# Output-projection weights and two mixers' outputs kept as split pairs, linear attention woven into projections, token halves

## The chip, the cores and the metric

One Trainium2 chip, one core of it. Five engines work from queues of their own, each in its own fixed order: PE (matrix products), DVE (vector), ACT (scalar), POOL (GpSimd), SP (which here issues the DMAs). The metric is device microseconds of one launch; the median of the runs is compared.

## What is computed

One layer of a streaming encoder on 1024 tokens of width 1024, all fp32.

```python
h = rmsnorm(x, ln1)
z = h @ w_in                      # split among three token mixers
y_pool = pool_mixer(u_pool, w_pool, pool_scale)        # trailing means over 2, 4, 8, 16, minus identity, a product per group
y_gla  = gla_mixer(gq, gk, gv, gg, ga, w_a_up, b_a, gla_gn)   # gated linear attention, 4 heads of 64, chunks of 64
y_fox  = fox_mixer(fq, fk, fv, ff, b_f)                # softmax attention with forgetting, 8 heads of 64, causal
x = x + concat(y_pool, y_gla, y_fox) @ w_o             # widths 256, 256, 512
h = rmsnorm(x, ln2)
gate, up = split(h @ w_gu); x = x + (silu(gate) * up) @ w_down
return rmsnorm(x, ln_f)
```

In the linear attention, per head: `S_t = diag(alpha_t) S_{t-1} + k_t^T v_t`, `o_t = q_t S_t`, by chunks: products within a chunk (`att = q_in k_in^T`, masked, times v), and q times the state before the chunk; then a normalisation per head and a gate `silu(g)`.

## The kernel before

Each large fp32 matrix product runs as three products of a split pair: an operand is rounded to a form that PE takes at full rate (`hi`, by ACT), the remainder (`lo`) is a subtraction (DVE or POOL), and PE adds hi·hi, hi·lo and lo·hi (`gemm`, L138). `split_w` (L111 to L113) loads and splits a weight; `load_w` uses buffers of small rings, `load_g` large ones. Names end in `h` and `l` for the two parts.

A scheduler orders each engine's queue by its own model of time, within the dependencies and within the buffers: tiles from `G` share large SBUF slots that are handed out again in order of release (`free`), tiles from `R` sit in rings, PSUM banks belong to tags (`s`, `pt`, `o`, `gm`). Code order is a priority, not the final order.

The stages, with the microseconds of the profiled execution:

- 0 to 72: first norm, transposes into `hT`, gates (`psg`), the pool mixer's input projections `zp0`, `zp1`.
- 72 to 118: keys and queries of the linear attention (`gla_qk`): projections `zgk0`, `zgq0`, `zgk1`, `zgq1`, 48 products of 512 columns each (`project`, L253). DVE and POOL prepare decays `bc`, `d1`, `d2`; `pk` turns the keys.
- 118 to 203: the pool mixer's sums (`ps`, `pd`) and products `py`; `gla_state` (small products `pkv`, L325, and the running state `St` on DVE, L330); values of the attention `psv0`; `gla_out` per head pair: gate projection `zgg`, scores `pat` (L353), masked into `attb` (L355), outputs `po` (L364 within a chunk, L368 with the state), normalisation `on`, turn `pot`, gate `gy`. Outputs go to DRAM (`mixd`) in fp32.
- 203 to 498: forgetting attention, four head pairs p = 0 to 3 (`fox_item`: scores `s`, softmax `pb` with the scaling L499 on POOL, turns `pt` L510, `pp`, outputs `o` L524), with the projections `zq`, `zk`, `psv1` in between, and for p = 3 the first half of the output projection, `pxa` (k = 0 to 3: pool and linear attention's outputs), as filler. `load_mix` reads rows of `mixd` into `mr` and splits them (ACT L562, POOL L563). `w_o` is loaded and split here: k = 0 to 3 with POOL, the rest with DVE. `fb` tiles hold the forget sums of one head.
- 498 to 560: second half `pxb` (k = 4 to 7), residual, second norm, its turns `n2pt` (L639).
- 560 to 977: gate and up products (L710, tiles `m`) by a scheme of seven products for a 2 by 2 block product; `left` prepares the left factors `hA`, `right` the weights, `start` begins a column block.
- 977 to 1202: down products (L916, `d`), again seven; POOL combines weights (`rw`, L808), which ACT and DVE split (`hw`, `lw`, L815, L816); at the end `final` normalises the tiles `c0` to `c7` and stores them (L883 to L887), and frees them.

Of the kernel before, what the change touches and what calls it, by code (L numbers as in the profile page):

```python
# [9 lines left out]
F32 = mybir.dt.float32  # L10
# [21 lines left out]
def tile_hybrid_block(ctx: ExitStack, tc, x, w_fv, w_gv, w_zt, w_o, w_gu, w_down, ln, w_pool, w_a3, chans, b_f, consts, out):  # L32
# [107 lines left out]


# [118 lines left out]
    decs, bcs = [], []  # L260
# [24 lines left out]
    def gla_qk(j):  # L285
        bc = bcs[j]
        b3 = e3(bc)
        dc = cst.tile([P, 16], F32, name=f"dec{j}")
        decs.append(dc)
        ACT.activation(dc, b3[:, :, 63], AF.Exp, scale=1.0 / 16)  # L290
        d1, d2, eq = G(f"d1_{j}"), R(f"d2_{j}"), G(f"eq{j}")
        POOL.tensor_tensor(out=e3(d1), in0=b3, in1=b3[:, :, 31:32].broadcast_to([P, 16, 64]), op=ALU.subtract)
        POOL.tensor_tensor(out=e3(d2), in0=b3[:, :, 63:64].broadcast_to([P, 16, 64]), in1=b3, op=ALU.subtract)
        ACT.activation(eq, d1, AF.Exp, scale=1.0 / 16)
        ACT.activation(d1, d1, AF.Exp, scale=-1.0 / 16)
        ACT.activation(d2, d2, AF.Exp, scale=1.0 / 16)
        ACT.activation(bc, bc, AF.Exp, scale=1.0 / 16)
        k_, q_ = R(f"gk{j}"), R(f"gq{j}")
        for csl, ps in project(8 + 2 * j, f"zgk{j}"):
            ACT.activation(k_[:, csl], ps, AF.Copy)  # L300
        DVE.tensor_tensor(out=d2, in0=k_, in1=d2, op=ALU.mult)
        DVE.tensor_tensor(out=d1, in0=k_, in1=d1, op=ALU.mult)
        for csl, ps in project(9 + 2 * j, f"zgq{j}"):
            ACT.activation(q_[:, csl], ps, AF.Copy, scale=0.125)
        DVE.tensor_tensor(out=eq, in0=q_, in1=eq, op=ALU.mult)
        POOL.tensor_tensor(out=bc, in0=q_, in1=bc, op=ALU.mult)
        kt = G(f"k2t{j}")
        for h in range(2):
            pt = PS("pt", f"pk{j}_{h}")
            for i in range(4):  # L310
                tb = 4 * h + i
                PE.transpose(pt[:, i * P:(i + 1) * P], d2[:, tb * P:(tb + 1) * P], ident)
            ACT.activation(kt[:, h * 512:(h + 1) * 512], pt, AF.Copy)
        return eq, d1, bc, kt

    def gla_state(j, kt):

        St = G(f"St{j}")
        POOL.memset(St[:, 0:64], 0.0)
        ps = [PS("s", f"pkv{j}_{q}") for q in range(2)]  # L320
        for n in range(15):
            tb, r = n // 2, slice(64 * (n % 2), 64 * (n % 2) + 64)
            o = ps[n % 2][:, (n // 2) * 64:(n // 2) * 64 + 64]
            for a in range(2):
                PE.matmul(o[64 * a:64 * a + 64], kt[r, tb * P + 64 * a:tb * P + 64 * a + 64],  # L325
                          gv[tb // 4][r, (tb % 4) * 256 + (2 * j + a) * 64:(tb % 4) * 256 + (2 * j + a + 1) * 64],
                          start=True, stop=True)
        for n in range(15):
            o = ps[n % 2][:, (n // 2) * 64:(n // 2) * 64 + 64]
            DVE.scalar_tensor_tensor(out=St[:, (n + 1) * 64:(n + 2) * 64], in0=St[:, n * 64:(n + 1) * 64],  # L330
                                     scalar=decs[j][:, n:n + 1], in1=o, op0=ALU.mult, op1=ALU.add)
        free(f"k2t{j}")
        return St

# [4 lines left out]
    def gla_out(j, qi, ki, qe, St):  # L339
        sg = R(f"sg{j}")  # L340
        for csl, ps in project(12 + j, f"zgg{j}"):
            ACT.activation(sg[:, csl], ps, AF.Silu)
        y = R(f"gy{j}")
        for c in range(2):
            pat = [PS("pt", f"pat{j}_{c}_{a}") for a in range(2)]
            po = [PS("s", f"po{j}_{c}_{a}") for a in range(2)]
            ab = attb[c]
            for i in range(4):
                tb = 4 * c + i
                tsl = slice(tb * P, (tb + 1) * P)  # L350
                for a in range(2):
                    r = slice(64 * a, 64 * a + 64)
                    PE.matmul(pat[a][:, i * P:(i + 1) * P], ki[r, tsl], qi[r, tsl], start=True, stop=True)  # L353
            for a in range(2):
                DVE.copy_predicated(ab[:, a * 512:(a + 1) * 512].rearrange("p (m t) -> p m t", t=P),  # L355
                                    gmask.rearrange("p (o t) -> p o t", o=1).broadcast_to([P, 4, P]),
                                    pat[a].rearrange("p (m t) -> p m t", t=P))
# [15 lines left out]
            for a in range(2):  # L373
                ACT.activation(o4[:, a], pv[a], AF.Square)
# [634 lines left out]
```

## Time and profile before

| what | value |
|---|---|
| median of three runs | 1199.56 us (1198.48 to 1200.44) |
| the profiled execution's own time | 1203.56 us |
| its span in the profile | 1201.8 us |
| granted PE clock, mean | 0.979 of full |
| busy: PE, PE weight loads, DVE, ACT, POOL | 1159.9, 974.8, 810.2, 530.9, 390.9 us |
| DMA | 126.34 MB, mean 105 GB/s |
| chain that ended last | PE 84%, DVE 5%, DMA 3%, issue 3%, POOL 3%, ACT 2% |

Busy time of PE is the time between a product's start and its modelled end: at half clock it counts the same work as twice the time. A row of a table of stages gives the length, the busy time of each engine with its count of instructions, the granted clock, the busy share of the DMA engines and GB/s. A row of the timeline gives start, length, engine, line, operation, tiles. A row of the waits says which engine waited for what: total, times, longest.

### The profile page before, as it was taken

What the parts mean: (1) busy time and instruction counts of PE and PEld (TensorE: products, weight loads), DVE (VectorE), ACT (ScalarE), POOL (GpSimd) and SP (SyncE); (2) the same over time, 40 slices, a digit from 0 to 9 for tenths busy, and PEclk for the clock granted to TensorE, in tenths of its full rate; (3) what the DMA queues carried; (4) which work ended last, traced back from release to release, by engine and by line L of the source; (5) the groups of instructions that cost most, each with busy time, mean ns of one, the idle gap of its engine ahead of it and who ended that gap; (6) DMA issues with size and microseconds to landing.
All of it is one profiled execution on the core that took longest, in us unless ns stands there. A gap on an engine that the chain in (4) does not pass through costs nothing.

```text
span 1201.8 us, 15933 instructions
## 1 busy us (share of the span) xinstructions
PE 1159.9 (97%) x5928; PEld 974.8 (81%) x5928; DVE 810.2 (67%) x1328; ACT 530.9 (44%) x965; POOL 390.9 (33%) x285
## 2 busy tenths in 40 slices
PE   6999999999999989899999999999999999999995
PEld 6878788889988778777888888888888888888874
DVE  7567612278748676468998768676776685766674
ACT  6362121257656745346444334443343344334353
POOL 2163122243333823331022220122202270660873
PEclk9999889899999999899999999999999999999998
DMA  6121111111122522221153331323224588333223
GB/s 244 35 71 53 54 35 53 36 55 47 47 62 77 169 91 97 79 105 53 53 155 112 111 120 65 131 93 118 95 90 148 214 322 288 109 96 118 63 97 140
DMA packets 53565, 126.34 MB, mean 105 GB/s; under 512 B 4792, under 2 KB 10344, under 8 KB 53488
## 3 DMA queue, kind: packets, MB, share of 16 engines
q1 hardware_dynamic: 53056, 123.75, 30.7%
q0 software_dynamic: 432, 1.57, 0.4%
q8 instruction: 46, 0.75, 0.3%
q14 instruction: 31, 0.25, 0.1%
HBM read 93.03 MB, written 32.28 MB: 104 GB/s over the span
## 4 chain that ended last, share of the span: by engine, by line
PE 84%; DVE 5%; DMA 3%; issue 3%; POOL 3%; ACT 2%; POOLq 0%; SPq 0%; ACTq 0%; DVEq 0%
PE m L710 35%; PE d L916 16%; PE pxa L138 4%; PE psv L138 3%; PE o L524 3%; PE pt L510 2%; PE s L484 1%; PE zq0p L138 1%; PE zgg0p L138 1%; PE s L485 1%; DMA mr<-mixd 1%; PE psg L138 1%; PE po L364 1%; PE zq3p L138 1%; PE zgg1p L138 1%
## 5 line engine op out<-in xcount | busy, mean ns | idle before, releaser
L710 PE MATMUL m<-hA_0h,wr 128*128 128x512 f32 x616 | 214.3, 390 | 0.6 <-ACT hr L641 0.5
L710 PE MATMUL m<-hA_1h,wr 128*128 128x512 f32 x616 | 214.6, 389 | 0.0
L710 PEld LDWEIGHTS m<-hA_0h,wr 128*128 128x128 f32 x616 | 115.6, 188 | 24.9 <-ACT hr L641 1.1
L710 PEld LDWEIGHTS m<-hA_1h,wr 128*128 128x128 f32 x616 | 115.7, 188 | 23.9
L916 PE MATMUL d<-hw,ha 128*128 128x512 f32 x308 | 120.0, 392 | 5.3 <-ACT hw L815 5.3
L710 PE MATMUL m<-hA_0l,wr 128*128 128x512 f32 x308 | 119.9, 389 | 1.7 <-DVE hA_0l L671 1.7
L916 PE MATMUL d<-lw,ha 128*128 128x512 f32 x308 | 120.4, 391 | 0.8 <-DVE lw L816 0.8
L710 PE MATMUL m<-hA_1l,wr 128*128 128x512 f32 x308 | 119.8, 389 | 0.0
L762 POOL TENSOR_TENSOR cg<-cu,cu 128x512 f32<-128x512 f32 x11 | 19.2, 1742 | 308.7 <-DVE cu L739 308.7
L916 PE MATMUL d<-hw,la 128*128 128x512 f32 x308 | 118.8, 391 | 0.0
L694 ACT ACTIVATE wr<-ws 128x512 fp32r<-128x512 f32 x110 | 69.5, 631 | 109.2 <-DVE ws L693 54.9
L695 DVE TENSOR_TENSOR wr<-ws,wr 128x512 fp32r<-128x512 f32 x110 | 75.9, 696 | 26.0 <-ACT wr L694 26.0
L816 DVE TENSOR_TENSOR la<-ra,ha 128x1024 fp32r<-128x1024 f32 (+1 forms) x42 | 58.2, 1392 | 29.0 <-ACT ha L815 21.5
L808 POOL TENSOR_TENSOR rw<-wd,wd 128x512 f32<-128x512 f32 x33 | 56.4, 1737 | 51.3 <-PE d L916 46.6
L916 PEld LDWEIGHTS d<-hw,ha 128*128 128x128 f32 x308 | 58.1, 189 | 17.8 <-ACT hw L815 5.7
L710 PEld LDWEIGHTS m<-hA_0l,wr 128*128 128x128 f32 x308 | 57.8, 188 | 14.2 <-DVE hA_0l L671 2.2
L916 PEld LDWEIGHTS d<-lw,ha 128*128 128x128 f32 x308 | 58.3, 189 | 13.3 <-DVE lw L816 1.2
L815 ACT ACTIVATE ha<-ra 128x1024 fp32r<-128x1024 f32 (+1 forms) x42 | 41.2, 987 | 61.6 <-DMA ra<-cd 56.0
L916 PEld LDWEIGHTS d<-hw,la 128*128 128x128 f32 x308 | 58.1, 189 | 12.1
L710 PEld LDWEIGHTS m<-hA_1l,wr 128*128 128x128 f32 x308 | 57.8, 188 | 12.1
L499 POOL TENSOR_TENSOR pb<-pb,rl 128x128 f32<-128x128 f32 (+3 forms) x32 | 38.1, 1196 | 83.4 <-DVE rl L496 66.5
L816 DVE TENSOR_TENSOR lw<-rw,hw 128x1024 fp32r<-128x1024 f32 (+1 forms) x30 | 45.7, 1535 | 27.3 <-ACT hw L815 27.2
(391 smaller groups left out, 2764.1 us busy)
## 6 DMA issues: line engine op xcount, KB each, us to landing
ra<-cd SPq DMA_DIRECT2D x35, 512.0 KB, 3.7
wu<-in_w_gu_dram SPq DMA_DIRECT2D x22, 512.0 KB, 4.3
wg<-in_w_gu_dram SPq DMA_DIRECT2D x22, 512.0 KB, 3.7
wd<-in_w_down_dram SPq DMA_DIRECT2D x22, 512.0 KB, 6.5
cd<-cg SPq DMA_DIRECT2D x11, 512.0 KB, 4.6
cd<-cs SPq DMA_DIRECT2D x11, 512.0 KB, 6.2
cd<-cu SPq DMA_DIRECT2D x11, 512.0 KB, 7.5
fb<-Fd SPq DMA_DIRECT2D x8, 512.0 KB, 4.5
```

The lines of the kernel that those rows point to most:

```text
L138: PE.matmul(ps, a, b, start=(n == 0), stop=(n == last))
L499: POOL.tensor_tensor(out=pb[:, 0:W], in0=pb[:, 0:W], in1=rl[:, 0:1].broadcast_to([P, W]), op=ALU.mult)
L510: PE.transpose(pt[:, o0:o0 + P], Pb[i][:, (2 * n + b) * P:(2 * n + b + 1) * P], ident)
L524: PE.matmul(*args, start=(kb == 0 and n_ == 0), stop=(last and n_ == 1))
L694: ACT.activation(hi, src, AF.Copy)
L695: e2.tensor_tensor(out=lo, in0=src, in1=f(hi), op=ALU.subtract)
L710: PE.matmul(ps, a, b, start=(n == 0), stop=(n == 11))
L762: POOL.tensor_tensor(out=t_[:, 0:512], in0=a11, in1=a12, op=ALU.add)
L808: POOL.tensor_tensor(out=raw_[:, j * 512:j * 512 + 512], in0=wd[h0, j0 + j][:, e0, :], in1=wd[h1, j0 + j][:, e1, :], op=op)
L815: ACT.activation(hi[:, sl], src, AF.Copy)
L816: DVE.tensor_tensor(out=lo[:, sl], in0=src, in1=f(hi[:, sl]), op=ALU.subtract)
L916: PE.matmul(banks[t], a[:, o], b[:, ns], start=(j0 + j == 0 and m == 0), stop=(j0 + j == NF // 2 - 1 and m == 2))
```

## The change

Five things.

1. Linear attention is written as a class `Gla` per head pair, whose small operations (turned keys, state, scores, outputs, turned outputs) are handed to the following projections and emitted between their terms (`woven`). The weights' `lo` parts of these projections are made on DVE instead of POOL. The four `attb` products of a part of `po` come first, then the state's. `pool_tile` stands ahead in the code.
2. `keep_mix`: the outputs of pool and linear attention are split once and stored as pairs (`mixs`); `load_mix` for k < 4 only loads.
3. `keep_wo`: the eight row blocks of `w_o` are loaded, split and stored as pairs (`wod`) after the first attention values in the code; `fetch_wo` loads pairs later.
4. Token halves: a half is now tokens 0 to 511 or 512 to 1023 (before: 0 to 255 with 512 to 767, and the others). The last head pair runs its query blocks in the order 1, 0, 3, 2 (before 3, 1, 2, 0). `pxb` goes through the token blocks 0 to 7; at block 4 the first left factors and the first column block of the FFN are started, and the rings of `wr` and `w` are given up earlier.
5. `free(f"c{tb}")` at the end of `final` is gone.

```diff
+    def woven(ps, terms, smalls=()):
+        done = 0
+        for i, ((ah, al), (bh, bl)) in enumerate(terms):
+            for n, (a, b) in enumerate(((ah, bh), (ah, bl), (al, bh))):
+                PE.matmul(ps, a, b, start=(i == 0 and n == 0), stop=(i == len(terms) - 1 and n == 2))
+            while done < len(smalls) and (done + 1) * len(terms) <= (i + 1) * len(smalls):
+                smalls[done]()
+                done += 1
...
+    def keep_mix(k, y):
+        hi, lo = R(f"mh{k}", F32R), R(f"ml{k}", F32R)
+        ACT.activation(hi, y, AF.Copy)
+        DVE.tensor_tensor(out=lo, in0=y, in1=f(hi), op=ALU.subtract)
+        SP.dma_start(mixs[k, :, 0], f(hi))
+        SP.dma_start(mixs[k, :, 1], f(lo))
+
+    def keep_wo(k):
+        hi, lo = load_g(w_o[k * P:(k + 1) * P, :], f"wos{k}", tag="G")
+        SP.dma_start(wod[k, :, 0], f(hi))
+        SP.dma_start(wod[k, :, 1], f(lo))
+        free(f"wos{k}h", f"wos{k}l")
+
+    def fetch_wo(k):
+        hl = G(f"wo{k}h", F32R), G(f"wo{k}l", F32R)
+        for h in range(2):
+            SP.dma_start(f(hl[h]), wod[k, :, h])
+        return hl
...
-    g0 = gla_qk(0)
-    g1 = gla_qk(1)
     pool_tile(1, us[1])
     pool_tile(0, us[0])
     free("misc")
-    st0 = gla_state(0, g0[3])
-    st1 = gla_state(1, g1[3])
-    V = fox_values(0)
-    gla_out(0, g0[0], g0[1], g0[2], st0)
-    gla_out(1, g1[0], g1[1], g1[2], st1)
+    A = Gla(0)
+    A.keys()
+    A.queries(((), A.turn_keys()))
+    A.gates((A.state(), A.within(0)))
+    B = Gla(1)
+    B.keys((A.within(1) + A.outputs(0), A.outputs(1) + A.turned(0)))
+    B.queries((A.turned(1), B.turn_keys()))
+    B.gates((B.state(), B.within(0)))
+    o_ = [B.outputs(0), B.outputs(1)]
+    V = fox_values(0, (B.within(1), o_[0][:1], o_[0][1:], o_[1][:1], o_[1][1:] + B.turned(0), B.turned(1), (), ()))
+    for k in range(8):
+        keep_wo(k)
...
-        for a, m in ([(a, m) for a in range(2) for m in range(4)] if p < 3 else [(a, m) for m in (3, 1, 2, 0) for a in range(2)]):
+        for a, m in ([(a, m) for a in range(2) for m in range(4)] if p < 3 else [(a, m) for m in (1, 0, 3, 2) for a in range(2)]):
...
-        o0 = (tb // 4) * 256 + (tb % 2) * P
+        o0 = (tb % 4) * P
...
-    ws = [load_g(w_o[k * P:(k + 1) * P, :], f"wo{k}", eng=POOL) for k in range(4)]
+    ws = [fetch_wo(k) for k in range(4)]
...
-    mixes = [load_mix(4, g) for g in (1, 0)][::-1]
-    for tb in (2, 3, 6, 7, 0, 1, 4, 5):
...
+    for tb in range(NT):
+        if tb == 2:
+            mixes[1] = load_mix(4, 1)
+        if tb == 4:
+            free(*[f"mix{k}_0" for k in range(4, 8)])
+            for i in (3, 5):
+                left(i, *lefts[i])
+            first.append(start(0))
+        out_proj(tb, xs[tb], mixes[tb // 4], ws, "pxb")
...
-        free(f"c{tb}")
```

In the rows below, the number at a name's end tells tiles apart, and `xN` is a run of N alike. PE, early in the linear attention, before: the last products of `zgk0p1` are followed by `zgq0p0`.

```order
L138 MATMUL zgk0p1_867<-hT3_1_0_97,zgk0h_836 128x512
L138 MATMUL zgk0p1_867<-hT3_1_1_98,zgk0h_836 128x512
L138 MATMUL zgk0p1_867<-hT3_1_0_97,zgk0l_837 128x512
L138 MATMUL zgq0p0_901<-hT0_0_0_83,zgq0h_896 128x512
L138 MATMUL zgq0p0_901<-hT0_0_1_84,zgq0h_896 128x512
L138 MATMUL zgq0p0_901<-hT0_0_0_83,zgq0l_897 128x512
```

After:

```order
L146 MATMUL zgk0p1_922<-hT3_1_0_97,zgk0h_891 128x512
L146 MATMUL zgk0p1_922<-hT3_1_1_98,zgk0h_891 128x512
L146 MATMUL zgk0p1_922<-hT3_1_0_97,zgk0l_892 128x512
L500 MATMUL py1_0_842<-pd1_837,misc_70 128x512
L500 MATMUL py1_1_845<-pd1_837,misc_70 128x512
L146 MATMUL zgq0p0_958<-hT0_0_0_83,zgq0h_953 128x512
L146 MATMUL zgq0p0_958<-hT0_0_1_84,zgq0h_953 128x512
```

The two products `py1` of the pool mixer, before at the place of 128 us, now stand between the two projections. On DVE, what stands ahead of `pd1`, which they read; before, from the row of `d2_0` on:

```order
L301 TENSOR_TENSOR d2_0_825<-gk0_833,d2_0_825 128x1024
L302 TENSOR_TENSOR d1_0_824<-gk0_833,d1_0_824 128x1024
L399 COPY ps2_1_1114<-u1_763 128x1
L400 TENSOR_TENSOR ps2_1_1114<-u1_763 128x1023
L305 TENSOR_TENSOR eq0_826<-gq0_834,eq0_826 128x1024
L399 COPY ps4_1_1117<-ps2_1_1114 128x2
L400 TENSOR_TENSOR ps4_1_1117<-ps2_1_1114 128x1022
L399 COPY ps2_0_1139<-u0_704 128x1
L400 TENSOR_TENSOR ps2_0_1139<-u0_704 128x1023
```

After, from the second scan on:

```order
L311 SCALAR_TENSOR_TENSOR bc1_699<-reset_653,la1_675 128x1024
L113 TENSOR_TENSOR zgq0l_954<-zgq0r_952,zgq0h_953 128x1024
L480 TENSOR_TENSOR ps2_1_824<-u1_765 128x1023
L479 COPY ps4_1_827<-ps2_1_824 128x2
L480 TENSOR_TENSOR ps4_1_827<-ps2_1_824 128x1022
L479 COPY ps8_1_830<-ps4_1_827 128x4
L480 TENSOR_TENSOR ps8_1_830<-ps4_1_827 128x1020
L479 COPY ps16_1_833<-ps8_1_830 64x8
L480 TENSOR_TENSOR ps16_1_833<-ps8_1_830 64x1016
L491 COPY ps8_1_830<-ps16_1_833 64x1024
L493 SCALAR_TENSOR_TENSOR pd1_837<-ps8_1_830,misc_70,u1_765 128x1024
```

The pool's sums follow the scan and the split `zgq0l` directly, with `pd1` in the same run. PE, one of the new groups (`zgk1p0` is the projection of the second pair's keys); before, a part of the same outputs in `zgg0`'s projection:

```order
L364 MATMUL po0_0_0_1566<-gv0_112,attb0_654 128x64
L368 MATMUL po0_0_0_1566<-St0_1158,bc0_695 64x64 x2
L364 MATMUL po0_0_1_1567<-gv0_112,attb0_654 128x64
L368 MATMUL po0_0_1_1567<-St0_1158,bc0_695 64x64 x2
L364 MATMUL po0_0_0_1566<-gv0_112,attb0_654 128x64
L368 MATMUL po0_0_0_1566<-St0_1158,bc0_695 64x64 x2
L364 MATMUL po0_0_1_1567<-gv0_112,attb0_654 128x64
L368 MATMUL po0_0_1_1567<-St0_1158,bc0_695 64x64
L138 MATMUL zgg0p0_1511<-hT0_0_0_83,zgg0h_1506 128x512
L138 MATMUL zgg0p0_1511<-hT0_0_1_84,zgg0h_1506 128x512
L368 MATMUL po0_0_1_1567<-St0_1158,bc0_695 64x64
```

After:

```order
L409 MATMUL pat0_1_0_1170<-eq0_882,d1_0_880 128x128
L409 MATMUL pat0_1_1_1171<-eq0_882,d1_0_880 128x128
L428 MATMUL po0_0_0_1194<-gv0_112,attb0_656 128x64
L428 MATMUL po0_0_1_1195<-gv0_112,attb0_656 128x64
L428 MATMUL po0_0_0_1194<-gv0_112,attb0_656 128x64
L428 MATMUL po0_0_1_1195<-gv0_112,attb0_656 128x64
L434 MATMUL po0_0_0_1194<-St0_1024,bc0_697 64x64 x2
L434 MATMUL po0_0_1_1195<-St0_1024,bc0_697 64x64 x2
L434 MATMUL po0_0_0_1194<-St0_1024,bc0_697 64x64 x2
L434 MATMUL po0_0_1_1195<-St0_1024,bc0_697 64x64 x2
L146 MATMUL zgk1p0_1163<-hT3_0_1_96,zgk1h_1158 128x512
L146 MATMUL zgk1p0_1163<-hT3_0_0_95,zgk1l_1159 128x512
```

A group is now four and eight `po` products of one part, with two products of the projection before the next group. At the end of the output projection PE's row now holds twelve products each of the FFN's first tiles `m0_3` and `m1_3` between the products of `pxb6`, `pxb7` and the last turns `n2pt6`, `n2pt7`; before, FFN products came in only after `n2pt4`, ahead of and behind `n2pt5`. POOL in the last stage, before:

```order
L808 TENSOR_TENSOR rw6_6_10220<-wd0_7_8946,wd1_7_8657 128x512
L808 TENSOR_TENSOR rw6_8_10257<-wd0_8_8984,wd1_8_8659 128x512
L808 TENSOR_TENSOR rw6_8_10257<-wd0_9_8986,wd1_9_8676 128x512
L878 TENSOR_TENSOR c0_8864<-c0_8864,lnfb_9255 128x512
L878 TENSOR_TENSOR c1_8866<-c1_8866,lnfb_9255 128x512
L101 TENSOR_TENSOR f0_r_10127<-f0_v_10126,mhalf_76 128x1
L878 TENSOR_TENSOR c2_8868<-c2_8868,lnfb_9255 128x512
L101 TENSOR_TENSOR f1_r_10140<-f1_v_10139,mhalf_76 128x1
L878 TENSOR_TENSOR c3_8870<-c3_8870,lnfb_9255 128x512
L101 TENSOR_TENSOR f2_r_10153<-f2_v_10152,mhalf_76 128x1
L101 TENSOR_TENSOR f3_r_10166<-f3_v_10165,mhalf_76 128x1
L808 TENSOR_TENSOR rw6_10_10294<-wd0_10_9024,wd1_10_8678 128x512
```

After:

```order
L865 TENSOR_TENSOR rw6_4_10233<-wd0_4_8954,wd1_4_8686 128x512
L865 TENSOR_TENSOR rw6_4_10233<-wd0_5_8956,wd1_5_8688 128x512
L865 TENSOR_TENSOR rw6_10_10344<-wd0_10_9074,wd1_10_8728 128x512
L865 TENSOR_TENSOR rw6_2_10152<-wd0_2_8897,wd1_2_8667 128x512
L865 TENSOR_TENSOR rw6_2_10152<-wd0_3_8899,wd1_3_8684 128x512
L865 TENSOR_TENSOR rw6_6_10270<-wd0_6_8994,wd1_6_8705 128x512
L865 TENSOR_TENSOR rw6_6_10270<-wd0_7_8996,wd1_7_8707 128x512
L865 TENSOR_TENSOR rw6_8_10307<-wd0_8_9034,wd1_8_8709 128x512
L865 TENSOR_TENSOR rw6_8_10307<-wd0_9_9036,wd1_9_8726 128x512
```

The combination `rw6_10` stood behind the last `c` tiles and now stands ahead of `rw6_2`. On SP, where nothing of the row is shown, 18 loads of 512 KB (pairs of `w_o`, pairs of mixes, `xa`), from `wo0h` on, stand ahead of the load `fb3_1`, which before stood after `wo0r`, `wo1r`, four `xa` and six halves of `mr`.

More of the change, by code (lines that the diff above doesn't have):

```diff
@@ L283, in decays @@
         free("fx")
[L285 to L333, printed above, removed]
@@ L643, in norm2 @@
         free(f"n2sq{tb}")
-    mixes = [load_mix(4, g) for g in (1, 0)][::-1]
-    for tb in (2, 3, 6, 7, 0, 1, 4, 5):
-        g = (tb // 2) % 2
-        out_proj(tb, xs[tb], mixes[g], ws, "pxb")
-        SP.dma_start(x3d[tb], xs[tb])
-        norm2(tb, xs[tb])
-        free(f"xa{tb}")
-        if tb in (7, 5):
-            free(*[f"mix{k}_{g}" for k in range(4, 8)])
-    free("wo6h", "wo6l", "wo7h", "wo7l", "ln2b")
-    idle.extend(rings.pop("wr") + rings.pop("w"))
-    hA = {}
-    def left(i, in0, in1=None, op=None):
-        hA[i] = []
-        for kp in range(2):
-            hi, lo = (G(f"hA{i}_{kp}{h}", F32R).rearrange("p (k t) -> p k t", k=2) for h in "hl")
-            src = raw[in0][kp]
-            if in1 is not None:
-                t_ = G(f"hs{i}{kp}").rearrange("p (k t) -> p k t", k=2)
-                DVE.tensor_tensor(out=t_, in0=src, in1=raw[in1][kp], op=op)
-                src = t_
-                free(f"hs{i}{kp}")
-            ACT.activation(hi, src, AF.Copy)
-            DVE.tensor_tensor(out=lo, in0=src, in1=f(hi), op=ALU.subtract)
-            hA[i].append((hi, lo))
     cd = dpool.tile([7, NF // 2, P, 512], F32, name="cd")
@@ L823, in prep, with left @@
             ready.append(ops)
+    hA = {}
+    def left(i, in0, in1=None, op=None):
+        hA[i] = []
+        for kp in range(2):
+            hi, lo = (G(f"hA{i}_{kp}{h}", F32R).rearrange("p (k t) -> p k t", k=2) for h in "hl")
+            src = raw[in0][kp]
+            if in1 is not None:
+                t_ = G(f"hs{i}{kp}").rearrange("p (k t) -> p k t", k=2)
+                DVE.tensor_tensor(out=t_, in0=src, in1=raw[in1][kp], op=op)
+                src = t_
+                free(f"hs{i}{kp}")
+            ACT.activation(hi, src, AF.Copy)
+            DVE.tensor_tensor(out=lo, in0=src, in1=f(hi), op=ALU.subtract)
+            hA[i].append((hi, lo))
     seen = []
@@ L841, in tile_hybrid_block @@
              6: (2, 0, ALU.subtract)}
-    first = [start(fi) for fi in range(2)]
+    mixes = [load_mix(4, 0), None]
+    first = []
+    for tb in range(NT):
[7 more added lines that the diff above has]
+        out_proj(tb, xs[tb], mixes[tb // 4], ws, "pxb")
+        SP.dma_start(x3d[tb], xs[tb])
+        norm2(tb, xs[tb])
+        free(f"xa{tb}")
+    free(*[f"wo{k}{h}" for k in range(4, 8) for h in "hl"], "ln2b", *[f"mix{k}_1" for k in range(4, 8)])
+    first.append(start(1))
     for i in (3, 5, 4, 1, 2, 7, 6):
-        left(i, *lefts[i])
+        if i not in (3, 5):
+            left(i, *lefts[i])
         if i == 7:
```

220 lines of the change are left out of this document (149 added, 71 removed).

## The prediction

> **What bounds the kernel now.** I read the stages first, then the granted clock, the waits of the PE queue, the chain at the end. The stages, one row each: length, busy time of PE, PEld, DVE, ACT, POOL with instruction counts, granted clock, DMA share, GB/s.
>
> ```profile
> 72.00:125.00 53.00, 52.50 (x266) 44.15 (x265) 33.30 (x23) 20.11 (x28) 30.44 (x12) 1.00 0.21 65
> 125.00:165.00 40.00, 38.11 (x356) 31.84 (x355) 19.53 (x58) 9.14 (x23) 3.39 (x3) 0.91 0.08 32
> 165.00:240.00 75.00, 75.00 (x385) 59.66 (x386) 15.67 (x29) 13.83 (x23) 18.23 (x12) 0.86 0.16 50
> 240.00:400.00 160.00, 159.72 (x1035) 144.38 (x1034) 116.50 (x293) 98.54 (x212) 60.78 (x55) 1.00 0.20 61
> 400.00:430.00 30.00, 25.00 (x135) 21.11 (x134) 21.20 (x49) 19.22 (x36) 22.37 (x17) 0.89 0.49 163
> 430.00:500.00 70.00, 64.22 (x364) 55.14 (x363) 43.28 (x89) 32.21 (x69) 19.27 (x20) 0.98 0.25 82
> 500.00:560.00 60.00, 57.28 (x272) 46.17 (x270) 39.84 (x52) 30.73 (x66) 23.96 (x23) 0.97 0.28 101
> 560.00:977.00 417.00, 416.42 (x1838) 344.50 (x1837) 319.84 (x481) 177.90 (x294) 85.05 (x59) 1.00 0.36 119
> 1176.00:1202.00 26.00, 13.43 (x52) 10.33 (x50) 10.22 (x17) 8.30 (x17) 5.91 (x8) 0.83 0.42 158
> ```
>
> PE is busy nearly everywhere, so time can be won in two ways only: where PE stands idle (length less busy: 1.9 us in 125–165, 13.5 us in 400–560, 12.6 at the end) and where its clock is below 1.00. In 165–240 PE is never idle, yet runs at 0.86. The windows that lie wholly inside the slow stretches (length, PE busy, clock, DMA share, GB/s):
>
> ```profile
> 128.40:135.20 6.80, 6.80 (x19) 0.50 0.00 0
> 166.00:176.20 10.20, 10.20 (x38) 0.50 0.33 98
> 206.90:217.20 10.30, 10.30 (x41) 0.50 0.01 2
> 408.30:411.70 3.40, 3.40 (x17) 0.50 1.01 365
> 425.40:428.80 3.40, 3.40 (x16) 0.50 0.51 170
> 497.00:503.90 6.90, 5.39 (x15) 0.51 0.01 3
> 1183.10:1186.50 3.40, 3.07 (x7) 0.50 0.00 0
> ```
>
> The clock is full or half, in steps of about 3.4 us. Linear attention holds 27.3 us at half clock: 13.7 us lost. 400–560 holds 13.7 us: 6.9 lost. The tail loses 1.7.
>
> What precedes a drop: before 166 the last 2.1 us are only the alternating L364/L368 products (columns: start, length, engine, operation).
>
> ```profile
> 162.46 0.33 PE L364 MATMUL po<-gv,attb 128*128 128x64 f32 x2
> 164.24 0.43 PE L364 MATMUL po<-gv,attb 128*128 128x64 f32 x2
> 164.60 0.33 PE L368 MATMUL po<-St,bc 64*64 64x64 f32 x2
> ```
>
> PE counts as busy there, and the clock falls all the same. [...]
>
> The waits of PE that the change touches (total, times, longest), and the tail's chain:
>
> ```profile
> PE d L916 <- ACT hw L815: 5.3, 1, 5.3
> PE pxb L138 <- ACT mix L562: 2.8, 1, 2.8
> PE pat L353 <- DVE ps L414: 1.9, 1, 1.9
> ...
> 1178.97 2.04 DMA out_dram<-c
> 1181.45 1.27 POOL rw L808
> 1183.43 11.27 PE d L916 x42
> ```
>
> The last 42 products wait for a weight combination whose buffer is a c tile still being stored.
>
> **The change, part by part.**
>
> *Linear attention woven into projections.* It adds no products. Long runs of small ones are cut into groups of 8 to 16 between 12 or more dense ones, so most windows hold dense work. One stretch stays poor: 8 pat and 12 po products, two dense ones, 12 po more. I take one drop of 6.8 us there (3.4 lost), so of 13.7 us lost, 10.3 come back. Bounds: 13.7 (no drop), 0 (all drops stay). [...] The small products themselves I leave at 0: their count is unchanged, the new order has fewer kind changes inside a group and more around it; bounds ±2, a tenth of 32 pairs at about 0.63 us (from 162.46 to 164.24 there are three pairs, 0.6 each). The 1.9 us wait of pat goes, since dense work now stands ahead of it: +1.9.
>
> *The pool's products come early.* This is a new wait. In PE's row py1 now stands between zgk0p and zgq0p; PE cannot pass it. The rows that price it:
>
> ```profile
> 74.17 3.91 DVE L277 TENSOR_TENSOR_SCAN bc<-reset,la 128x1024 f32<-128x1024 f32 x1
> 81.72 0.57 ACT L300 ACTIVATE gk<-zgk0p 128x512 f32<-128x512 f32 x1
> 83.49 0.62 PE L138 MATMUL zgq0p<-hT,zgq0h 128*128 128x512 f32 x2
> 83.98 1.90 POOL L293 TENSOR_TENSOR d<-bc 128x1024 f32<-128x1024 f32 x1
> 88.02 1.04 ACT L112 ACTIVATE zgk1h<-zgk1r 128x1024 fp32r<-128x1024 f32 x1
> 119.00 1.21 DVE L400 TENSOR_TENSOR ps<-ps 64x1016 f32<-64x1016 f32 x1
> 120.24 3.29 DVE L305 TENSOR_TENSOR eq<-gq,eq 128x1024 f32<-128x1024 f32 x1
> 126.38 1.28 DVE pd L413
> ```
>
> PE reaches py1 at 83.3. DVE must first end the second scan (78.1 in this run; a POOL operation beside it had stretched it, one split of 1.2 comes ahead: about 78), then do the split zgq0l, four ps sums (five times 1.21), a copy (half of that, an estimate), pd (1.28) and small pieces (0.3, an estimate): 8.2 us, so 86 undisturbed. Meanwhile POOL runs three operations of 1.90; beside POOL an operation of 1.21 took 3.29 (eq), so up to 5.7 more: 92. I take 89, the middle, since the third POOL operation can start when the sums are nearly done: PE idles 5.5 us. Then zgq0p needs the bank of zgk0p, and its evacuation (gk, 0.57) now stands on ACT behind the second py copy (0.57) and the split mh1 (1.04): 2.2 more. An idle stretch of that length costs the clock a window, 1.7. Sum −9.4; bounds −4.5 and −15. The py products leave 128–137, where PE waited only for pat, so nothing is given back there. [...]
>
> *Output weights and mixes kept as pairs.* Added ahead of 240: eight loads that move, 16 stores of 512 KB, eight ACT splits at 1.04, eight DVE splits at 1.21, four mix splits on each. DVE is busy 15.7 of 75 us in 165–240 and ACT 13.8: hidden; if that cover goes, it is the slower rival below. The stores and the DMA share of 0.08 to 0.20 there: hidden too. Six more weight splits go from POOL to DVE; only the early one matters, counted above. Later, 16 loads of pairs replace eight of weights. Removed in 400–560: the lo splits on POOL, which stand ahead of the scaling L499 that attention waits for, and the mix splits.
>
> ```profile
> 418.18 2.38 POOL L113 TENSOR_TENSOR wo3l<-wo3r,wo3h 128x1024 fp32r<-128x1024 f32 x1
> ...
> 382.48 1.59 PE zk3p L138 x7
> 399.94 2.08 PE zk3p L138 x9
> 425.44 4.33 DMA mr<-mixd
> 491.96 5.85 DMA mr<-mixd
> ```
>
> 400–430 loses 5.0 idle and 3.4 of clock. Four splits of 2.38 go and so does the first wait on mr. But 18 loads of 512 KB (9.4 MB, 26 us at the 365 GB/s of 408–412) now stand ahead of fb3_1 on SP; they follow zk3's products, which release the buffers one by one from 382 to 402, so with 26 us of transfer fb3_1 lands up to 8 us late, with pxa products standing ahead of it on PE. I take 5.4 of 8.4 (bounds −4 and 8.4).
>
> *Token halves.* At 491–504 PE waits for mr, then its split, and the clock falls: 5.8 idle in 430–500 and 3.4. Blocks 3 and 2 end now the attention; the last load (mr6) still takes a buffer that only frees when attention is nearly over, and its 5.85 is followed by ACT and POOL as before. I give back 1.5 of 9.2 (bounds −3 and 7). In 500–560, 2.7 us idle: the FFN's first products now stand between the last blocks' projections and their transposes, so they fill it, and a little of the clock: 2.5 (bounds 0 and 3).
>
> *The c tiles are not released.* The last combination no longer gets a c tile, and is moved ahead of rw6_2 on POOL. The 5.3 us wait and the 1.7 of clock go; one combination and its split come ahead of others on POOL and DVE, cost 1. Gain 6.0 (bounds 3 and 7).
>
> *Forgetting attention, 240–400*: PE idles 0.3 of 160 us and the change takes nothing from it; 0 (bounds ±2).
>
> **Sum.** 10.3 + 1.9 − 9.4 + 5.4 + 1.5 + 2.5 + 6.0 = 18.2. The profiled execution took 1203.56 (span 1201.8), which gives 1185.4; it lay 4.0 above the median of the runs, 1199.56, against which the forecast is 1181.
>
> **Rivals.**
>
> *Most of the waste goes.* For it: none of the lost time is work, and in the new rows dense products stand ahead of nearly every late operand. If the early stall is at its lower bound (+4.9), the clock stays full in linear attention (+3.4) and 400–500 gives back 11 instead of 6.9 (+4.1), the time is 1169; with all bounds on that side, 1159. Against: the DVE chain ahead of pd is serial and its length is in the rows.
>
> *The clock does not stay up.* Small groups still fill enough of the windows, or the new waits open gaps, and the drops move without becoming fewer: the 10.3 stay lost, 1191. For it: the row at 162–164 needed only about 2.1 us of small products in a 3.4 us window. Against: in the new order about 3.2 us of dense products (12, at the 0.27 us of the last 42 in the tail's row) stand between nearly all groups.
>
> *The woven groups wait on DVE; the kernel gets slower.* One mechanism: eight w_o splits and six GLA splits now share DVE with the state updates, masks and normalisations that the next small group on PE waits for, and PE, in order, cannot go round a small group as it could when the long projections stood elsewhere. Price: if each of the eight w_o splits delays a group by what an operation takes beside POOL, 8 × 3.29 = 26.3 us, the time is 1207. It decides at 18.2 / 8 = 2.3 us a split. For it: the sums of 1.21 that became 3.29. Against: DVE 15.7 busy of 75 us, and in the new DVE row no two w_o splits stand side by side.
>
> *Little of it counts.* Early stall at −15 and the burst of loads at −4: 1199.56 − (18.2 − 5.6 − 9.4) = 1196, still just faster; with one more drop of the clock it is no change.
>
> **Chances.** The forecast with sizes within 1172 to 1188: 0.55. Most of the waste goes: 0.15. The clock does not stay up: 0.10. Little of it counts: 0.08, of which 0.04 within 0.2% (2.4 us, about what a measurement of this kernel tells from no change). Slower by woven waits: 0.12, of which 0.01 within 0.2%. So faster 0.84, same 0.05, slower 0.11. The range leaves out the farthest of the first rival and the slower cases: 1164 to 1198.
>
> **What would show it.** After: a wait of PE of 4 to 8 us for pd near 84–90, followed by one of about 2 for an ACT evacuation, then a short half clock; 72–240 otherwise at a granted clock of 0.95 or more (0.92 over it now, from the rows above), with no wait of pat. Combinations on POOL in 395–420 without splits; PE idle in 400–500 down from 10.8 to 5 to 7 us, with a wait for mr's split left near the end of attention. FFN products before the last transposes, under 1 us idle there. At the end no wait of the down products for the last combination, and a dense run to the end of products. The prediction is wrong if PE waits for py by 15 us or more, if it waits repeatedly in 100–200 for DVE results behind a w_o split, or if the clock record still shows three stretches at half.

## The result, and the profile after

The changed kernel takes 1178.59 us (median of 4 runs, 1177.12 to 1180.34), the kernel before beside it 1199.02: a ratio of 0.9823, 95% interval 0.98 to 0.9845, 20.4 us less. The forecast was 1181, with 18.2 us less. The profiled execution of the changed kernel took 1177.12, span 1175.4; that of before has a span of 1201.8. So the two traces differ by 26.4 us, 6.0 more than the medians: the profiled execution of before took 1203.56, 4.5 above the median here, and that of the changed kernel lay 1.5 below its own. The sums below are of the traces.

The stages of the changed kernel, as in the prediction (length, busy time of PE, PEld, DVE, ACT, POOL, granted clock, DMA share, GB/s):

```profile
72.00:125.00 53.00, 46.25 (x245) 34.47 (x244) 37.57 (x47) 23.33 (x30) 12.76 (x5) 0.94 0.20 71
125.00:165.00 40.00, 40.00 (x295) 32.81 (x294) 21.49 (x28) 11.30 (x17) 9.05 (x4) 1.00 0.51 180
165.00:240.00 75.00, 73.14 (x524) 64.23 (x524) 32.06 (x70) 27.47 (x52) 22.24 (x17) 1.00 0.45 158
400.00:430.00 30.00, 30.00 (x173) 26.16 (x172) 20.03 (x50) 12.20 (x29) 3.75 (x4) 1.00 0.31 97
430.00:500.00 70.00, 64.62 (x357) 54.50 (x356) 39.28 (x73) 30.85 (x66) 21.39 (x22) 0.98 0.33 116
500.00:560.00 60.00, 55.41 (x257) 45.89 (x256) 50.55 (x58) 34.58 (x66) 13.95 (x13) 0.94 0.19 71
```

In 125 to 240, where the clock stood at 0.91 and 0.86, it is full; the loss has moved to 72 to 125, where PE now idles 6.8 us at 0.94. 400 to 430 has neither idle time nor half clock any more; 500 to 560 got worse (4.6 idle against 2.7). The windows at half clock and the waits of PE:

```profile
87.40:90.80 3.40, 3.36 (x4) 0.50 0.00 0
94.20:97.60 3.40, 3.40 (x9) 0.50 0.62 252
479.90:483.30 3.40, 3.40 (x9) 0.50 0.36 77
537.90:544.70 6.80, 5.80 (x17) 0.50 0.00 0
```

```profile
PE n2pt L725 <- DVE n2sq L720: 4.6, 1, 4.6
PE py L500 <- DVE pd L495: 4.4, 1, 4.4
PE pxb L138 <- ACT mix L644: 2.8, 1, 2.8
PE zgq0p L146 <- ACT gk L344: 2.4, 1, 2.4
```

Four stretches are left, two of them right behind the new wait for pd and for the bank of zgk0p. No wait for the last weight combination stands in the list any more.

Where the traces part, by landmarks on PE: the span from the last product of zgk0p to the first of zq1p (the linear attention, the first values, zq0 and zk0 in both) shrinks from 83.3–239.3 to 82.7–226.5, by 12.2 us. From there to the last product of zk3p both take 162.3. From there to the first down product: 575.4 and 567.4, 8.0 less. The down products: from 217.3 to 209.2; what follows the last of them: from 7.5 to 10.0; so the tail has 5.6 less.

### The profile page after: what moved, and what is told of

Same layout as the page of the kernel before. It is cut to its first block, busy times and chain, and to the rows that moved or that the text cites. A ratio compares the mean times of both kernels' runs of the same rounds, so it can differ in the third digit from the quotient of the medians.

```text
span 1175.4 us, 16005 instructions
## 1 busy us (share of the span) xinstructions
PE 1136.0 (97%) x5928; PEld 958.5 (82%) x5928; DVE 827.2 (70%) x1342; ACT 531.3 (45%) x961; POOL 353.7 (30%) x267
## 4 chain that ended last, share of the span: by engine, by line
PE 75%; DVE 3%; issue 1%; POOL 1%; DMA 1%; ACT 1%; POOLq 0%; ACTq 0%; DVEq 0%; SPq 0%
PE m L767 35%; PE d L1007 15%; PE pxa L138 3%; PE o L604 3%; PE pxb L138 3%; PE psv L146 2%; PE pt L590 2%; PE s L564 1%; PE s L565 1%; PE zq3p L146 1%; PE zk1p L146 1%; PE zq2p L146 1%; PE zk3p L146 1%; PE zq1p L146 1%; PE zk0p L146 1%
## 5 line engine op out<-in xcount | busy, mean ns | idle before, releaser
L819 POOL TENSOR_TENSOR cg<-cu,cu 128x512 f32<-128x512 f32 x11 | 19.6, 1778 | 306.8 <-DVE cu L796 306.8
L573 ACT ACTIVATE pb<-pb,mn 128x128 f32<-128x128 f32 (+3 forms) x64 | 49.5, 774 | 34.1 <-DVE mn L569 33.9
```

The lines of the kernel that those rows point to most:

```text
L573: ACT.activation(pb[:, 0:W], pb[:, 0:W], AF.Exp, bias=mn[:, 0:1], scale=-1.0, accum_out=l[:, i:i + 1])
```

## The experiments

The runs came in three groups of four kernels. Each group stood beside runs of the kernel before on the same chip (its medians there: 1196.7, 1198.8 and 1196.2), and each ratio is to these. Two kernels of different groups can be compared by their times or by their ratios; the two ways differ by some 4 us, and where it matters both are given.

**The pool tiles behind the keys.** The two `pool_tile` calls moved:

```diff
-    pool_tile(1, us[1])
-    pool_tile(0, us[0])
     A = Gla(0)
     A.keys()
+    pool_tile(1, us[1])
+    pool_tile(0, us[0])
```

> The changed kernel with the two pool tiles written behind the first keys' projection, so that PE's row has zgq0p directly behind zgk0p and py behind zgq0p. Theory (the early stall is the cost of py standing there, 4.4 + 2.4 us idle and two windows at half clock, 10 us in all): 1167 to 1171, no wait for pd, no half clock between 80 and 100. Rival (the sums on DVE are only late somewhere else, since DVE and ACT have the same work): the wait moves to pk, py or pat and 1175 to 1179 is measured.

Measured: 1180.63, ratio 0.9862 (0.9847 to 0.9877), no faster than the changed kernel and 1.6 above the rival's range. The rival held in kind: PE's wait moved along. Its row in the list of waits, and DVE's and PE's rows there (start, length, operation, idle time before and its releaser):

```profile
PE py L500 <- DVE pd L495: 6.2, 2, 3.4
```

```profile
95.98 1.28 DVE L493 SCALAR_TENSOR_TENSOR pd<-ps,misc,u 128x1024 f32<-128x1024 f32 x1 [4.43 <-PE pk L369]
...
98.74 3.51 PE L500 MATMUL py<-pd,misc 128*128 128x512 f32 x4 [2.81 <-DVE pd L495]
...
105.68 1.22 PE L500 MATMUL py<-pd,misc 128*128 128x512 f32 x1 [3.42 <-DVE pd L495]
```

But not for the rival's reason. DVE itself idles 4.43 us before pd: in this order pd is written into the ring buffer that d2_0 leaves only when PE has turned the keys (pk). Moving the calls in the code changed who gets which buffer.

**The pool tiles behind the queries**, one step further:

```diff
-    pool_tile(1, us[1])
-    pool_tile(0, us[0])
     A = Gla(0)
     A.keys()
     A.queries(((), A.turn_keys()))
+    pool_tile(1, us[1])
+    pool_tile(0, us[0])
```

> The changed kernel with the two pool tiles written behind the queries, so that py1 stands inside the gate projection zgg0, some 20 us behind the end of zgk0p instead of directly behind it, and the keys' and queries' own DVE work comes ahead of the last sums. Theory (as the run with the pool tiles behind the keys showed, the length of the DVE chain sets the wait; with 20 us of dense products ahead it is covered): no wait for pd above 1 us, no half clock between 80 and 115, 8 to 11 us faster than the unchanged one beside it. Rival (DVE is behind all through this stage, and the next small group waits as long): within 3 us of the unchanged one, with the waits of py or pat at 4 us or more together.

Measured: 1170.94 (1168.06 to 1172.89), ratio 0.9754 (0.9712 to 0.9795), 7.2 us under the changed kernel run beside it, a little less than the 8 to 11 expected. No wait of py is left and PE is full where the new stall was:

```profile
72.00:125.00 53.00, 52.89 (x312) 40.95 (x311) 40.83 (x50) 26.18 (x34) 14.63 (x5) 1.00 0.30 105
125.00:165.00 40.00, 40.00 (x304) 32.85 (x303) 21.30 (x35) 13.48 (x18) 11.52 (x5) 1.00 0.49 179
```

This is the fastest version of all that were run. The changed kernel beside these three:

> The changed kernel once more, unchanged, as the measure for the three beside it on this chip. Expected at 0.980 to 0.985 of the kernel before, 1174 to 1180.

Measured: 1178.10, ratio 0.9818 (0.9771 to 0.9864).

**The po products alternating again**, in the changed kernel:

```diff
                 for i, a in both:
                     h = 2 * j + a
                     PE.matmul(po[a][:, i * 64:i * 64 + 64], attb[c][:, (4 * a + i) * P:(4 * a + i + 1) * P],
-                              gv[c][:, i * 256 + h * 64:i * 256 + (h + 1) * 64], start=(i == 0), stop=False)
-                for i, a in both:
+                              gv[c][:, i * 256 + h * 64:i * 256 + (h + 1) * 64], start=True, stop=False)
                     r = slice(64 * a, 64 * a + 64)
                     for q in range(2):
...
-                                  self.St[r, n * 64:(n + 1) * 64], start=False, stop=(i == 3))
+                                  self.St[r, n * 64:(n + 1) * 64], start=False, stop=True)
```

> The changed kernel with the po products of a part in the alternating order of before (one within the chunk, two with the state, and so on), nothing else. Theory (the grouping by kind is worth the 6.8 us by which the po products shrank between the two traces): 1184 to 1187, po's two lines together near 19 us. Rival (the prediction's: the order of kinds is worth nothing, the rest came from the clock): 1177 to 1180.

Measured: 1187.46, ratio 0.9917 (0.9898 to 0.9936), 9 to 11 us over the changed kernel (by time and by ratio), and just above the 1184 to 1187 expected. The edit also changes the start and stop marks of the products, which go with the order; they were not run apart from it. The timeline of PE shows where the time goes. First a part of po in the changed kernel, four attb products (8 records) and eight state products (16), 1.43 us from 129.48 to 130.91; then the same in this run, from 182.18 on:

```profile
129.48 1.10 PE L428 MATMUL po<-gv,attb 128*128 128x64 f32 x8
130.52 0.46 PE L434 MATMUL po<-St,bc 64*64 64x64 f32 x16
130.91 0.50 PE L146 MATMUL zgk1p<-hT,zgk1h 128*128 128x512 f32 x1
```

```profile
182.18 0.33 PE L428 MATMUL po<-gv,attb 128*128 128x64 f32 x2
182.44 0.33 PE L433 MATMUL po<-St,bc 64*64 64x64 f32 x4
...
184.58 0.43 PE L428 MATMUL po<-gv,attb 128*128 128x64 f32 x2
...
185.20 0.38 PE L146 MATMUL psv<-wfv_0h,hT 128*128 128x256 f32 x1
```

```profile
182.20:185.60 3.40, 3.40 (x33) 1.00 0.92 300
185.60:189.00 3.40, 3.40 (x18) 0.50 0.07 29
```

One attb product with its two state products takes about 0.6 us alternating and 0.36 in the largest groups. Taken from each row's start to the next over all 32 of them, PE spends 19.6 us on po here and 12.5 in the changed kernel: 7.0 less for the grouping. (The busy times of po's two lines, which overlap, add up to 24.1 here, not to the 19 expected, and to 14.4 in the changed kernel.) And a window of 3.4 us that holds 3 us of alternating products, with PE never idle by the profile, is followed by one at half clock, which costs up to 1.7. In linear attention this is the only one outside the early stall: from 131.50 to 136.97 this kernel also alternates for 4.9 us, with 0.57 of dense work in between, and an attb product with its two state products keeps to the 0.63 us of full clock there (1.03 at half, by the rows of before). So even alternating, the woven groups lose one window where the kernel before had 27.3 us at half clock.

**The po products grouped, in the kernel before**, where they stand in long runs: the products themselves are those of the changed kernel's `outputs`.

```diff
-            for i in range(4):
-                tb = 4 * c + i
-                for a in range(2):
+            for i2 in range(2):
+                both = [(i, a) for i in (2 * i2, 2 * i2 + 1) for a in range(2)]
+                for i, a in both:
...
+                for i, a in both:
```

> The kernel before with its po products grouped by kind in parts of four and eight, all still in the long runs of before. Theory (two effects of the new linear attention that add: grouping by kind shortens the products by 7 us, and long runs of small products alone let the clock fall): 1190 to 1194, with the three stretches at half clock still there, 20 to 28 us in all between 120 and 220. Rival (the alternation itself makes the clock fall): at most one stretch stays and the time is 1180 to 1186. Second rival (grouping is worth nothing): 1197 to 1200.

Measured: 1189.12, ratio 0.9939 (0.9912 to 0.9966). The time lies 0.9 below the theory's range; the mechanism does not fit. In the profiled execution, which was the fastest of ten (1182.54), none of the three stretches is left, though the products still stand in runs (length, busy, clock):

```profile
120.00:165.00 45.00, 43.10 (x435) 37.45 (x434) 26.90 (x63) 12.20 (x28) 12.46 (x5) 1.00 0.14 49
165.00:222.00 57.00, 57.00 (x348) 47.41 (x347) 14.78 (x27) 10.99 (x19) 15.18 (x11) 1.00 0.16 56
```

Ten executions spread from 1182.54 at a mean clock of 0.991 to 1198.94 at 0.979. So grouping can save the clock without any weaving, and by the spread it does not always; no trace of a slower execution was kept. The four executions of the changed kernel lie within 3.2 us. Why a given execution loses the clock was not shown.

**The release of the c tiles put back**, at the end of `final` in the changed kernel:

```diff
             SP.dma_start(out[tb * P:(tb + 1) * P, ns], x2[:, ns])
+        free(f"c{tb}")
```

> The changed kernel with the release of the c tiles put back. Theory (this line alone is the tail's gain of about 6): 1183 to 1187, with a wait of 4 to 6 us of the last down products for the last combination and a window at half clock. Rival (the buffers fall in another order in the changed kernel, and the last combination gets another buffer): 1177 to 1180.

Measured: 1183.96, ratio 0.9895 (0.988 to 0.9909), 5.4 and 5.9 over the two measurements of the changed kernel by time, 8.6 and 9.2 by ratio: the theory. The wait is back as it was, `PE d` for the split of the last combination:

```profile
PE d L1008 <- ACT hw L872: 5.7, 1, 5.7
```

The down products take 217.5 us again (209.2 without the line), the rest 7.4 instead of 10.0.

**No pairs of output weights**, in the changed kernel:

```diff
-    for k in range(8):
-        keep_wo(k)
...
-    ws = [fetch_wo(k) for k in range(4)]
+    ws = [load_g(w_o[k * P:(k + 1) * P, :], f"wo{k}", eng=POOL) for k in range(4)]
...
-    ws = [fetch_wo(k) for k in range(4, 8)]
+    ws = [load_g(w_o[k * P:(k + 1) * P, :], f"wo{k}") for k in range(4, 8)]
```

> The changed kernel without the pairs of output weights in memory: loaded and split where the kernel before did it (k = 0 to 3 with POOL, the rest with DVE). Theory (the gain in 400 to 430, which was 8.4 us of idle and half clock and is 0 in the changed kernel, comes from these splits having left POOL and ACT): 6 to 10 us slower than the unchanged one, idle of PE back between the last zk3p and the end of the third head pair. Rival (the gain there comes from the new order of blocks and from the mix pairs): within 3 us.

Measured: 1179.86, ratio 0.9824 (0.9777 to 0.9872), 1.8 over the unchanged one beside it, with intervals that overlap: the rival. In the trace the splits do cost PE something there:

```profile
380.00:400.00 20.00, 19.25 (x119) 16.84 (x118) 16.51 (x35) 13.78 (x28) 14.24 (x14) 1.00 0.74 258
400.00:430.00 30.00, 28.05 (x167) 24.58 (x166) 23.42 (x58) 17.31 (x39) 10.16 (x9) 0.94 0.43 148
430.00:500.00 70.00, 66.88 (x361) 56.77 (x360) 38.76 (x71) 28.13 (x55) 19.62 (x19) 0.98 0.22 72
```

2.7 us of idle time and a window at half clock before 430, 4.4 us of the 8.4; after it 3.1 idle against 5.4 with the pairs. So about half of the local gain is the weight pairs', and half of that is lost again behind it.

**No pairs of the two mixers' outputs**, in the fastest version; `load_mix` treats k < 4 as it does the others:

```diff
     def keep_mix(k, y):
-        hi, lo = R(f"mh{k}", F32R), R(f"ml{k}", F32R)
-        ACT.activation(hi, y, AF.Copy)
-        DVE.tensor_tensor(out=lo, in0=y, in1=f(hi), op=ALU.subtract)
-        SP.dma_start(mixs[k, :, 0], f(hi))
-        SP.dma_start(mixs[k, :, 1], f(lo))
+        SP.dma_start(mixd[3 + k], y)
```

> The kernel with the pool tiles inside the gate projection (1170.9), without the pairs of the two mixers' outputs: stored in fp32 and split at load, as before, in the new token halves. Theory (with the weight pairs, these splits are what left POOL and ACT in 370 to 430; either alone is enough, the pairs are worth little): 1170 to 1174. Rival (the wait for mr at the start of pxa is back and with it a window at half clock): 1175 to 1181.

Measured: 1172.77, ratio 0.98 (0.9778 to 0.9821), 1.8 over it by time and 5.5 by ratio, with intervals that overlap. By time the theory held; the two kernels never ran on the same chip, and the worth of these pairs is not clear of noise.

**The linear attention's code of before, po grouped**, the rest as changed:

```diff
-    A = Gla(0)
-    A.keys()
...
+    g0 = gla_qk(0)
+    g1 = gla_qk(1)
+    pool_tile(1, us[1])
+    pool_tile(0, us[0])
+    free("misc")
+    st0 = gla_state(0, g0[3])
+    st1 = gla_state(1, g1[3])
+    V = fox_values(0)
+    gla_out(0, g0[0], g0[1], g0[2], st0)
+    gla_out(1, g1[0], g1[1], g1[2], st1)
     for k in range(8):
         keep_wo(k)
```

> The changed kernel with the linear attention's code of before (long runs of small products, weights split on POOL, pool tiles behind the queries), but with po grouped by kind; pairs, token halves and the unreleased c tiles stay as changed. Theory (the grouping does most of the linear attention's part, the weaving only guards the clock, and it paid 10 us for the early stall): 0 to 8 us faster than the unchanged one, with executions that differ by 5 to 12 us among each other as the clock falls or not. Rival (weaving itself is what gains): 5 to 15 us slower.

Measured: 1194.38, ratio 0.9951 (0.9925 to 0.9976), 16 slower than the changed kernel; ten executions within 5.1 us. The list of waits shows one that is in no other run, and the chain that ended last shows what stands behind it:

```profile
PE zk0p L146 <- DVE q L482: 14.6, 1, 14.6
```

```profile
206.85 4.83 DMA wos7r<-in_w_o_dram
...
218.26 6.93 DMA wod<-wos5h
...
225.27 0.60 ACT q L481
```

q waits for the store of a pair (wos5h), by the list of the chain; a buffer that the store has to leave would explain it. The chain runs through loads, splits and stores of the pairs one after the other. The next run tells whether the slowness is this or the code itself.

**The same without the pairs of output weights**, by the edit shown above for these:

> The run with the linear attention's code of before (po grouped, pool tiles behind the queries), without the pairs of output weights; to be read against the run of the changed kernel without these pairs (1179.9). Theory (there the 14.6 us wait of zk0p came from the traffic of the weight pairs, whose stores and loads stood ahead of q's operands on SP and ACT; without them the old code with grouped products is as good as the woven one that pays for its early stall): 1176 to 1184, no wait of zk0p, the clock falling in some executions. Rival (weaving itself gains, by what the long runs cost in waits and clock): 1188 to 1196.

Measured: 1177.29 (four executions within 2.1 us), ratio 0.9839 (0.9819 to 0.9859), against 1179.86 and 0.9824 for the woven code without these pairs. The theory held: in its present form, with the early stall, the woven code is no faster than the old one with grouped products. Without the stall it is. The table takes the same work of PE, from the last product of zgk0p to the first of zq1p, in the profiled executions (us):

| kernel | length | PE busy | at half clock |
|---|---|---|---|
| before | 156.0 | 153.6 | 27.3 |
| before, po grouped | 138.6 | 136.2 | 0 |
| old linear attention, po grouped, no weight pairs | 139.0 | 135.3 | 6.8 |
| changed, po alternating | 153.1 | 145.1 | 17.0 |
| changed | 143.8 | 135.2 | 6.8 |
| changed, pool tiles behind the queries | 135.5 | 133.7 | 0 |

Grouping without weaving brings the stretch to about 139; weaving as well, once the stall is out, to 135.5, some 3 us less. Weaving also leaves room in which the traffic of the pairs fits.

**The FFN started after the last token block**, in the fastest version:

```diff
         if tb == 4:
             free(*[f"mix{k}_0" for k in range(4, 8)])
-            for i in (3, 5):
-                left(i, *lefts[i])
-            first.append(start(0))
...
-    first.append(start(1))
+    first = [start(0), start(1)]
     for i in (3, 5, 4, 1, 2, 7, 6):
-        if i not in (3, 5):
-            left(i, *lefts[i])
+        left(i, *lefts[i])
```

> The same kernel (1170.9) with the first left factors and the first FFN column block started behind the last token block, as before. Theory (the early products fill waits at 515 to 535, but their loads hold up POOL in front of the last norms, a wait of 4.9 and two windows at half clock: both nearly cancel): 1169 to 1174. Rival (the early start is worth the 5 us of idle it was made for): 1175 to 1179.

Measured: 1174.74, ratio 0.982 (0.9791 to 0.9849), 3.8 over it by time, 7.9 by ratio: by time between the two expectations. The wait for the last norm is gone from its list, replaced by others (pxb 3.9, m 2.8).

**The first FFN block at token block 7**, in the fastest version:

```diff
             for i in (3, 5):
                 left(i, *lefts[i])
-            first.append(start(0))
+        if tb == 7:
+            first.append(start(0))
```

> The same kernel (1170.9) with the left factors at block 4 as changed, but the first FFN column block started at block 7, so that its weight splits come a little later on POOL, ACT and DVE. Theory (the wait of the last turns is for the second column block's load, which this does not move): within 2 us of 1170.9. Rival (fewer splits ahead of the norms of blocks 5 to 7 shorten it): 1165 to 1168.

Measured: 1174.16, ratio 0.9813 (0.9793 to 0.9832), 3.2 over by time, 7.1 by ratio: neither. Its trace has a window at half clock at 131.9 to 135.3 that the fastest version's profiled execution lacks, and the same wait of n2pt (5.3 against 4.9). So the later start does not shorten that wait, and part of the difference lies in another stage.

## Why the prediction came out right, and which terms were off

The total was met within 2.4 us, and most steps hold by their own measure, but the closeness is partly luck: two errors cancelled. The term for the small products was missing, some 8 us. The other way, the sum was worked out on a profiled execution of before that took longer than most, and was taken whole from the median: by the traces the kernels differ by 26.4 us, by the medians by 20.4. That execution's mean granted clock was 0.979, while 28 of the 32 executions of this kernel beside the experiments show 0.984 to 0.989, so part of the lost clock that the sum gave back is not lost in most executions. Which part, no trace shows.

*The clock in linear attention, +10.3:* measured 27.3 us at half clock before and 6.8 after. Counted as half lost, that is 13.7 and 3.4, so +10.3. The residue is not where the step put it: the stretch with 8 pat and 24 po products did not drop, and both windows lie behind the early stall. The reason that the step gave, dense work between the small groups, is borne out by the run with po alternating, but grouping alone can do the same, as the kernel before with po grouped shows; the step left it out. And half clock does not take twice the time for all products: in the trace of before, dense products of 512 columns stand 0.43 us apart in place of 0.23, but an attb product with its two state products takes 1.03 in place of 0.63. So the 27.3 us cost nearer 12 than 13.7, an estimate from these rows; busy time at half clock is not simply twice that at full.

*The small products, taken at 0 with bounds ±2:* this is the term that was mis-sized. The stage gained 12.2 us. 10.3 came from the clock, counted as above; idle time in 72 to 240 rose from 2.4 to 8.6, which takes 6.2. The other 8 are products that take less time, and the run with po alternating shows 7.0 of them directly. The step counted fewer kind changes inside a group as balanced by more around it; the rows above show three products in 0.6 us alternating and 0.36 in a large group. The rows of the trace of before had the alternating price but none of the grouped one, and a bound of a tenth had no row behind it.

*The wait of pat, +1.9:* it is gone, as forecast; zq0p (1.2) and the turn pot (0.7) wait for DVE in its place.

*The early stall, −9.4:* measured 4.4 us waiting for pd and 2.4 for the gk evacuation behind py and mh1, against 5.5 and 2.2, and two windows at half clock, which the step counted as one: up to 10.2 in all. Moving the pool tiles behind the queries removed both waits and both windows. The place and both causes are as forecast. pd was ready at 87.4 rather than 89: DVE had one operation stretched by POOL, not two. The rows of POOL and of DVE:

```profile
77.03 2.84 POOL L334 TENSOR_TENSOR d<-bc 128x1024 f32<-128x1024 f32 x1 [2.23 <-DVE bc L311]
78.00 2.95 DVE L480 TENSOR_TENSOR ps<-u 128x1023 f32<-128x1023 f32 x1
...
81.06 1.22 DVE L480 TENSOR_TENSOR ps<-ps 128x1022 f32<-128x1022 f32 x1
```

The sum of 2.95 ran beside POOL's operation; the next, of 1.22, ran while POOL idled. The upper end of the step, 92, at which all of POOL's 5.7 us would add, was not reached, since only one of its operations met the chain. POOL's operation was itself stretched, from 1.90 to 2.84. The copy, put at half of 1.21, took 0.69.

*400 to 430, +5.4 of 8.4:* all 8.4 went, but the named reason, the splits of the weights, is worth 4.4 in this stage by the trace without these pairs, and about 2 in the whole time (1179.86 against 1178.10). The worth of the mix pairs is not clear of noise, and the new order of the blocks, the other candidate, was not run alone: what gave the rest stays open. fb3_1 behind 18 loads cost PE nothing.

*The end of attention and the second norm, +1.5 and +2.5:* 430 to 500 idles 5.4 us with one window at half clock (9.2 us lost before, 7.1 now); 500 to 560 went the wrong way, 4.6 idle, where the step put 2.7 before and next to nothing after, and 6.8 at half clock. The FFN's early products do fill the waits they stand ahead of: starting them after the last block cost 3.8. But their second block's weights come late. POOL, in order, holds the norm of the last block but one (`n_r`) behind them, and DVE the residual and the norm of the last block behind their splits `wr`:

```profile
521.01 4.50 DMA wu<-in_w_gu_dram
...
525.65 2.98 POOL ws L750 x2
528.63 0.97 POOL n_r L101
...
531.86 2.98 DVE wr L752 x3
...
536.88 0.56 POOL n_r L101
...
537.46 1.30 DVE n2sq L720
...
538.89 1.94 PE n2pt L725 x8
```

Taken together, from zk3's end to the first down product, 8.0 us against 9.4 in the sum.

*The tail, +6.0:* 5.6: the down products take 8.1 less, what follows them 2.5 more, where the step put a cost of 1. Putting the line back alone brought the wait back.

*Forgetting attention, 0:* from zq1p to zk3p both take 162.3.

*The rivals.* That woven groups wait on DVE behind splits did not happen in this kernel. Its relative, that the pairs' traffic holds up something in order, did happen in the run with the old linear attention, at 14.6 us.

## What to carry to other kernels

Group small products by kind before weaving them anywhere: the order of kinds set their own time (an attb product with its two state products 0.6 us alternating, 0.36 grouped), and grouping alone could bring the clock back (from 27.3 us at half clock to none, in the one trace); weaving was worth some 3 us on top in the traces, and only once it no longer caused a stall. An operation that is moved early in an in-order row is paid for by the whole chain behind its operand (4.4 and 2.4 us of idle here), so move the row's work, not the operation, until the chain fits under dense products; and look which buffer the producer gets, since a later place can hand it one that is held (DVE idled 4.43 us ahead of pd). Splitting weights ahead into memory moved little time here (1.8 us), and its traffic can become the next wait (14.6 us with the old linear attention).

## What the runs showed of the hardware

The clock fell to half behind stretches in which the profile shows PE busy throughout (3.40 of 3.40 us): 162.5 to 165.9 before, 182.2 to 185.6 with alternating products. It was at half behind idle stretches of PE as well: 5.3 us up to 1183.4 before, 4.4 up to 87.4 and 4.6 up to 538.9 in the changed kernel; behind the 10.1 us at the start of the trace of before it was full (8.5 to 18.7). In the second, 3 us of alternating small products stood ahead of the drop, but such products did not bring one everywhere: the same kernel alternated likewise for 4.9 us between 131.50 and 136.97, with 0.57 of dense work in between, at the 0.63 us of full clock. In the changed kernel 2.75 us of grouped products with 0.57 of dense work between them (129.48 to 132.80) were followed by no drop either. What sets these cases apart was not shown.

At half clock not all products took twice the time: dense ones 1.9 times, an attb product with its two state products 1.6 times (0.23 to 0.43 and 0.63 to 1.03 us, in the trace of before).

A change from one kind of small product to the other cost about 0.16 us, an estimate that puts the whole difference between the two orders of po on it: 0.24 less for an attb product with its two state products, at 1.5 changes less.

Products of 128x512 of the split pairs start 0.23 us apart at full clock; one plain fp32 product of that size (`py`, two records) takes 1.06 (137.60 to 138.66, in the trace of before).

Where operations of DVE and POOL met, these rows of the trace of before show one or both of them longer: the second scan 3.91 us, beside POOL operations of 2.84 and 3.88, against 2.29 for the first scan alone and 1.94 and 1.90 for the like POOL operations alone; eq 3.29 beside POOL, against 1.21 for a product of the same size (L302) alone. A sum beside a POOL split kept its 1.21, and the split took 3.46, against 2.40 for one alone (79.73).
